# A hybrid gMLP and attention step on one core: the input projection in blocks of 512 columns, tiles at multiples of 512 bytes, and full rows for the last sample keys

## The chip, the cores and the metric

The kernel runs on one core of a Trainium2 chip. A core has a matrix engine (PE; its weight loads are shown apart as PEld), a vector engine (DVE), a scalar engine (ACT), a general engine (POOL) and a sync engine (SP) that here only starts DMAs. The metric is the device time of one execution in microseconds (us); lower is better. Several executions are timed and the median counts.

## The reference

One layer of a streaming encoder serves two groups with shared weights: a prompt of 2048 rows and 8 running streams with 16 new rows each, 128 sample rows in all. Model width is 1024, everything is fp32.

```python
h = rms_norm(x, norm_g)
z = einsum("btd,de->bte", h, w_in)                    # 1024 -> 3584 columns
u_a, v_a, g_a, q, k, v, g_b = split(z, 7 x 512)
y_a = u_a * spatial_gate(v_a) * silu(g_a)             # per 128-position chunk, lower-triangular mix, 4 heads
q, k = rms_norm(q), rms_norm(k)                       # per 64-wide half
a = softmax(Q1 K1) - lam * softmax(Q2 K2)             # 4 heads, ALiBi, block-causal in chunks of 64
y_b = rms_norm(a @ v) * silu(g_b)
y = x + concat(y_a, y_b) @ w_out
```

The prompt attends to itself. Each sample stream attends to 1024 cached keys and values and to its own 16 new ones. New keys, values and the sample's v_a rows are outputs too.

## The kernel before

**Precision.** Every fp32 operand of a product is split into a rounded high part and the rest (`split`, L136: one ACT copy, one subtraction on DVE or POOL). A product is three matmuls (`mm3`, L148): high by high, high by rest, rest by high.

**Token tiles.** Rows go in 17 tiles of 128: 0 to 15 are the prompt, 16 is the sample. `xload` and `xpose` load, normalize, transpose and split a tile into `xT`. Tiles 0 to 3 and 8 to 11 lie in the pool `p1g`, tiles 4 to 7 and 12 to 15 in the pool `p1`; the second half of the prompt takes the buffers of the first.

**Input projection.** The work is cut into 14 column blocks of 256: `v` (2), `qk` (4), `ug` and `vg` (4 each). `stream` takes all 14 blocks over tiles 0 to 7 and the sample, then all 14 over tiles 8 to 15. `load_w` (L287) brings a block's weights as 8 chunks of 128 rows by 256 columns: one DMA (two for `vg`), a scaled copy on ACT (L305), the rest on DVE (L306). Weight chunks have NW = 12 buffers, raw chunks three. `project` multiplies two token tiles by one block into one PSUM bank, 48 matmuls of 256 columns. The moving operand is the weight chunk, the stationary one is `xT`.

**Evacuation.** `qk_group`, `v_group`, `ug_group` and `vg_group` take a pair of tiles out of the bank. `vg_group` returns `finish`, the mixing product of the gMLP branch. `stream` calls the `finish` of a group of tiles right after the next group, whatever its kind. The `finish` of the sample tile appends its head to `gated_heads`.

**Order.** `weave` emits steps of two streams in a ratio of matrix-engine time that it counts in columns. The schedule is: 6 blocks of projection alone; then projection with the sample attention (ratio RS = 2.8); then, **once all four heads are in `gated_heads`**, `sample_finish` and the prompt attention of the first 8 tiles, called attention A, with projection (ratio RA = 2.0); then the output weights `wo`, in slots that attention A held; then what is left of the projection; then output projection with the attention of the other 8 tiles. A planner at compile time fixes the order of each engine's queue: it follows the order of emission, and takes a later instruction where, by its own estimate, an earlier one isn't ready.

**Attention A.** A unit is a head and a pair of query tiles, 16 units. `score_steps` cuts the keys with `chunks`: pieces of 512, except that a rest of 640 becomes 384 and 256. Exponentials of the first softmax have three buffers, of the second one. `value_steps` (L592) transposes them in PSUM (`a_tp`), splits them and multiplies (`oT`).

**Sample values.** `sample_values` multiplies 8 tiles of 128 keys and then the last 16 keys with two matmuls over 16 rows (`sO`, L830).

## Time and profile before

| | |
|---|---|
| median of 3 runs | 1416.73 us (1413.92 to 1419.37) |
| the profiled execution, from its first to its last instruction | 1410.9 us |
| what lies around it, against the median | 5.8 us |
| projection matmuls of 256 columns | 5376 on prompt tiles, 336 on the sample tile |
| output projection matmuls of 512 columns | 816 |
| mean granted clock of PE | 0.994 |

The profiled execution has no time of its own besides its span; a change of the span is carried to the median one to one. The page's slices are 35.3 us each. A matmul's shown duration includes its way through the array; the pace of a stream is found from a merged row of the timeline as (length minus one duration) over (count minus one).

### The profile page before, as it was taken

The page shows a single profiled execution, that of the slowest core. Times are in us where ns is not written, and L with a number is a line of the kernel's source. Part 1 is how long each engine was busy: PE and PEld are TensorE (multiplying, and loading weights), DVE is VectorE, ACT ScalarE, POOL GpSimd, SP SyncE. Part 2 cuts the span into 40 slices and gives each one's busy share as a digit, 9 for nine tenths or more (in the row PEclk, how much of TensorE's full clock was granted, in tenths as well). Part 3 has the DMA queues.
Part 4 walks back from the last instruction along what each step waited for, and adds up shares of the span by engine and source line. Part 5 has one row for each costly group of instructions (what it writes and reads, how often), then busy time and mean ns, then how long its engine had stood idle before and what let it go on. Part 6 is the DMA issues. An engine that isn't in the chain of part 4 may idle for free.

```text
span 1410.9 us, 27990 instructions
## 1 busy us (share of the span) xinstructions
PE 1360.5 (96%) x9892; PEld 1266.1 (90%) x9892; DVE 897.1 (64%) x2114; ACT 794.0 (56%) x1778; POOL 617.6 (44%) x796
## 2 busy tenths in 40 slices
PE   7999999999999989899999999988999999999998
PEld 6999999999999979899999999986888888888887
DVE  5442366767565764786766767444888778878632
ACT  5442356666655775565554655443777767667520
POOL 2361535555554655656232331243555545444310
PEclk9999999999999999999999999998999999999999
DMA  7533244545444476445343332166555433433223
GB/s 220 175 91 100 78 122 124 169 130 158 130 140 145 142 220 203 112 112 138 96 128 83 99 96 69 42 211 207 149 158 162 142 115 117 143 97 94 75 94 101
DMA packets 209245, 183.06 MB, mean 130 GB/s; under 512 B 21104, under 2 KB 167024, under 8 KB 209104
## 3 DMA queue, kind: packets, MB, share of 16 engines
q1 hardware_dynamic: 199280, 155.17, 36.9%
q0 software_dynamic: 9824, 26.09, 6.8%
q8 instruction: 78, 1.28, 0.4%
q14 instruction: 63, 0.52, 0.1%
HBM read 130.86 MB, written 42.47 MB: 123 GB/s over the span
## 4 chain that ended last, share of the span: by engine, by line
PE 50%; DMA 7%; DVE 5%; ACT 3%; issue 3%; POOL 3%; SPq 1%; ACTq 0%; DVEq 0%; POOLq 0%
PE acc L73 16%; PE oo L73 12%; PE S L73 8%; PE oT L73 7%; PE a_tp L77 4%; DMA wraw<-in_w_in_dram 2%; DMA svraw<-in_cache_v_dram 1%; DMA woraw<-in_w_out_dram 1%; DVE ex L584 1%; DMA x<-in_x_prompt_dram 1%; DVE ex L568 1%; PE y_tp L77 1%; DMA qraw<-q_scr 1%; POOL sv L139 1%; DVE w L306 1%
## 5 line engine op out<-in xcount | busy, mean ns | idle before, releaser
L73 PE MATMUL acc<-w,xT 128*128 128x256 f32 x5376 | 719.4, 284 | 2.5 <-DVE w L306 0.9
L73 PEld LDWEIGHTS acc<-w,xT 128*128 128x128 f32 x5376 | 676.2, 190 | 14.8 <-issue 2.7
L73 PE MATMUL oo<-wo,yT 128*128 128x512 f32 x816 | 223.6, 405 | 6.6 <-ACT yT L138 6.6
L73 PE MATMUL S<-kT,qT 128*128 128x512 f32 (+3 forms) x688 | 185.8, 367 | 6.2 <-DVE sst L568 3.9
L572 ACT ACTIVATE ex<-ex,sst 128x128 f32<-128x128 f32 (+15 forms) x128 | 153.9, 1203 | 61.0 <-DVE sst L568 59.5
L73 PEld LDWEIGHTS oo<-wo,yT 128*128 128x128 f32 x816 | 148.9, 191 | 34.7 <-ACT yT L138 7.6
L306 DVE SCALAR_TENSOR_TENSOR w<-wraw,normg,w 128x256 fp32r<-128x256 f32 x224 | 119.6, 555 | 87.1 <-ACT w L305 79.1
L305 ACT ACTIVATE w<-wraw,normg 128x256 fp32r<-128x256 f32 x220 | 105.8, 505 | 87.8 <-DMA wraw<-in_w_in_dram 75.3
L73 PE MATMUL oT<-aT,v 128*128 128x256 f32 x864 | 151.8, 290 | 2.9 <-ACT aT L138 1.9
L568 DVE CUSTOM_DVE_ANT_0 ex<-S,dist,sst 128x512 f32<-128x512 f32 (+2 forms) x192 | 123.2, 652 | 37.6 <-PE S L73 35.8
L73 PEld LDWEIGHTS oT<-aT,v 128*128 128x128 f32 x864 | 124.3, 189 | 14.5 <-DVE aT L139 3.9
L139 POOL TENSOR_TENSOR sv<-svraw,sv 128x512 fp32r<-128x512 f32 (+1 forms) x72 | 96.6, 1346 | 75.5 <-ACT sv L138 59.1
L73 PEld LDWEIGHTS S<-kT,qT 128*128 128x128 f32 x688 | 110.4, 191 | 21.3 <-DVE sst L568 8.6
L138 ACT CAST aT<-a_tp 128x512 fp32r<-128x512 f32 (+1 forms) x144 | 79.3, 559 | 70.4 <-PE a_tp L77 68.5
L139 DVE TENSOR_TENSOR aT<-a_tp,aT 128x512 fp32r<-128x512 f32 (+1 forms) x144 | 94.3, 658 | 38.2 <-ACT aT L138 37.3
L568 DVE CUSTOM_DVE_ANT_0 ex<-S,dist 128x512 f32<-128x512 f32 (+3 forms) x128 | 79.6, 629 | 29.8 <-PE S L73 16.6
L77 PE MATMUL a_tp<-ident,ex 128*128 128x128 f32 x544 | 83.1, 273 | 4.3 <-DVE ex L584 3.3
L784 POOL TENSOR_TENSOR slo<-slo,dist_s 64x256 f32<-64x256 f32 (+1 forms) x64 | 49.4, 772 | 63.3 <-ACT slo L783 60.5
L139 POOL TENSOR_TENSOR v<-vraw,v 128x512 fp32r<-128x512 f32 x36 | 48.2, 1338 | 54.5 <-ACT v L138 45.4
L77 PEld LDWEIGHTS a_tp<-ident,ex 128*128 128x128 f32 x544 | 63.3, 140 | 8.5 <-DVE gbt L641 1.9
L584 DVE SCALAR_TENSOR_TENSOR ex<-ex,sst 128x1024 f32<-128x1024 f32 (+4 forms) x64 | 65.1, 1038 | 1.1
L588 POOL TENSOR_TENSOR ex<-ex 128x1024 f32<-128x1024 f32 (+4 forms) x32 | 58.4, 1848 | 15.9 <-ACT ex L587 11.4
(144 smaller groups left out, 1925.5 us busy)
## 6 DMA issues: line engine op xcount, KB each, us to landing
wraw<-in_w_in_dram SPq DMA_DIRECT2D x160, 128.0 KB, 2.5
skraw<-in_cache_k_dram SPq DMA_DIRECT2D x64, 256.0 KB, 3.1
svraw<-in_cache_v_dram SPq DMA_DIRECT2D x64, 256.0 KB, 2.9
kT<-k_scr POOLq DMA_DIRECT2D x20, 512.0 KB, 4.6
vraw<-out_dram SPq DMA_DIRECT2D x36, 256.0 KB, 2.8
y<-y_scr SPq DMA_DIRECT2D x34, 256.0 KB, 3.0
out_dram<-xo SPq DMA_DIRECT2D x34, 256.0 KB, 2.1
wraw<-in_w_in_dram SPq DMA_DIRECT2D x128, 64.0 KB, 2.2
```

The lines of the kernel that those rows point to most:

```text
L73: pe.last = nc.tensor.matmul(*a, **k).ins
L77: pe.last = nc.tensor.transpose(*a, **k).ins
L138: act.copy(hi, src)
L139: (lo_eng or dve).tensor_tensor(out=lo, in0=src, in1=f(hi), op=ALU.subtract)
L305: act.activation(w[:, 0], r, AF.Copy, scale=normg[:, kc:kc + 1])
L306: dve.scalar_tensor_tensor(out=w[:, 1], in0=r, scalar=normg[:, kc:kc + 1], in1=f(w[:, 0]), op0=ALU.mult, op1=ALU.subtract)
L568: dve.tensor_tensor_reduce(out=ex[c][:, a:b], in0=s, in1=dist[:, off + a:off + b], scale=SLOPES[h], scalar=prev[c], op0=ALU.add, op1=ALU.m ...
L572: act.activation(ex[c][:, :w], ex[c][:, :w], AF.Exp, bias=prev[c], scale=-1.0, accum_out=st[:, c, 6:7])
L584: dve.scalar_tensor_tensor(out=p0, in0=p1, scalar=st[:, 1, 7:8], in1=p0, op0=ALU.mult, op1=ALU.add)
L588: pool.tensor_tensor(out=p0, in0=p1, in1=p0, op=ALU.add)
L784: pool.tensor_tensor(out=lo, in0=lo, in1=dist_s[rh, x:x + w_], op=ALU.add)
```

## The change

The column blocks become 512 wide: `v` for all heads (1 block), `qk` for two heads (2 blocks), `g` with u, v and both gates of one head (4 blocks). The first half runs v, qk, qk, g, g, g, g; the second v, qk, g, g, g, g, qk. One token tile by one block fills a bank: 24 matmuls of 512 columns. A weight chunk is 128 by 512, brought in two pieces, with 10 buffers instead of 12. Evacuation goes tile by tile. A `finish` is now kept in `keep["fin"]` and called by `fin()`: in `g_group` after the first tile of the next pair, and at the end of the stream. Small tiles go to a pool of their own ahead of the others, and slots are declared in an order with a filler of 480 bytes, so that the operands of most matmuls begin at multiples of 512 bytes. The 16 last sample keys are padded with zeros to 128 rows. `chunks` cuts plain pieces of 512. The last of the eight output weight chunks is loaded after the projection's pools are closed. Comment lines and docstrings are removed too.

```diff
-NW = 12             # weight chunks
+NW = 10
+    small = ctx.enter_context(tc.tile_pool(name="small", bufs=2, reuse_waits="tile"))
-    q_scr = [dtile([T + P, P], f"q_scr{h}") for h in range(H)]
+    q_scr = [dtile([T + P, 2, P], f"q_scr{hp}") for hp in range(H // 2)]
...
         def load_w(kind, h, res):
+            src = {"v": (lambda kc, i: win[kc, :, 5, 2 * i:2 * i + 2]),
+                   "qk": (lambda kc, i: win[kc, :, 3 + i, 2 * h:2 * h + 2]),
+                   "g": (lambda kc, i: win[kc, :, 0:2, h] if i == 0 else win[kc, :, 2:7:4, h])}[kind]
             for kc in range(8):
...
+                w = sb.tile([P, 2, 512], F32R, name="w", tag="w", bufs=NW)
+                for i in range(2):
+                    raw = (sb if progress[0] else at).tile([P, 2, P], F32, name="wraw", tag="wraw", bufs=3)
+                    sp.dma_start(raw, src(kc, i))
+                    r, cs = fl(raw), slice(i * 256, (i + 1) * 256)
+                    if i == 0 and not progress[0]:
+                        pool.tensor_scalar(out=w[:, 0, cs], in0=r, scalar1=normg[:, kc:kc + 1], scalar2=1.0,
+                                           op0=ALU.mult, op1=ALU.mult)
+                    else:
+                        act.activation(w[:, 0, cs], r, AF.Copy, scale=normg[:, kc:kc + 1])
+                    dve.scalar_tensor_tensor(out=w[:, 1, cs], in0=r, scalar=normg[:, kc:kc + 1],
+                                             in1=f(w[:, 0, cs]), op0=ALU.mult, op1=ALU.subtract)
...
+        def project(t, w, load):
             acc = bank("acc", "acc")
+            for kc in range(8):
+                mm3(acc, xTs[t][0][:, kc], xTs[t][1][:, kc], w[kc][:, 0], w[kc][:, 1], kc == 0, kc == 7)
+                next(load, 0)
+                sets[0] += 1
+                yield pe_time(1536) + (next(side[0], 0) if side and sets[0] % 3 == 0 else 0)
+            return acc
...
+        def g_group(h, tiles, w, loads):
+            sample = tiles[0] == NT
+            for pr in pairs(tiles):
...
+                for i, t in enumerate(pr):
+                    acc = yield from project(t, w, loads.pop(0))
...
+                    if i == 0:
+                        fin()
...
+                def finish(pr=pr, n=n, usg=usg, vhl=vhl):
...
+                    if sample:
+                        gated_heads.append(h)
+                keep["fin"] = finish
...
+            qkv = [("v", 0), ("qk", 0), ("qk", 1)]
+            gated = [("g", h) for h in range(H)]
+            kinds = qkv + gated, qkv[:2] + gated + qkv[2:]
...
-                    fin = yield from KIND[kind](h, g, w, loads)
-                    if keep.get("fin"):
-                        keep.pop("fin")()
-                    keep["fin"] = fin
+                    yield from KIND[kind](h, g, w, loads)
                 for _ in load:
                     pass
                 w = w_next
+            fin()
...
     def chunks(w, m=512):
-        res, x = [], 0
-        while w - x > m:
-            step = m - P if w - x == m + P else m
-            res.append((x, x + step))
-            x += step
-        res.append((x, w))
-        return res
+        return [(x, min(x + m, w)) for x in range(0, w, m)]
...
-            v = sa.tile([P, 2, 512], F32R, name="sv", tag="sv")[0:n]
-            split(raw, v[:, 0], v[:, 1], pool)
+            v = sa.tile([P, 2, 512], F32R, name="sv", tag="sv")
+            if n < P:
+                pool.memset(f(v), 0.0)
+            split(raw, v[0:n, 0], v[0:n, 1], pool)
...
+        pool.memset(f(aT[:, 8]), 0.0)
...
-                pe.matmul(o, lhsT=aT[0:n, kt].rearrange("p s q -> p (s q)"), rhs=vs[kt][:, i],
+                pe.matmul(o, lhsT=aT[:, kt].rearrange("p s q -> p (s q)"), rhs=vs[kt][:, i],
...
+        ctx.enter_context(tc.tile_pool(name="end", bufs=1, reuse_waits="tile", side="right")).tile(
+            [P, 120], F32, name="end", tag="end")
         bg = open_pool(right, "bg")
+        for tag, n in [(m[2], NK), (m[3], NK), (m[7], 1088), (m[11], 1088), ("dist", NK), (r[6], 544)]:
+            bg.tile([P, n], F32, name=tag, tag=tag, bufs=1)
...
-        while progress[0] < 5:
+        while progress[0] < 2:
...
-        while progress[0] < 6:
+        while progress[0] < 3:
...
-        for kc in range(8):
+        wo = [wo_tiles(wp, kc) for kc in range(7)]
+        for kc in range(7):
...
         left.close()
+        wo.append(wo_tiles(open_pool(right, "wo7", 1), 7))
+        for n in range(2):
+            raw = ypool.tile([P, 512], F32, name="woraw", tag="y", bufs=2)
+            sp.dma_start(raw, wout[7][:, n * 512:(n + 1) * 512])
+            split(raw, wo[7][n][:, 0], wo[7][n][:, 1], (pool, dve)[n])
```

231 lines of the change are left out of this document (82 added, 149 removed).

## The prediction

> **What bounds the kernel now.** I read the page first, then the busy time by stretches, then the timeline of PE, and last the timelines of ACT and SP where PE has holes. The page:
>
> ```profile
> PE 1360.5 (96%) x9892; PEld 1266.1 (90%) x9892; DVE 897.1 (64%) x2114; ACT 794.0 (56%) x1778; POOL 617.6 (44%) x796
> L73 PE MATMUL acc<-w,xT 128*128 128x256 f32 x5376 | 719.4, 284 | 2.5 <-DVE w L306 0.9
> ```
>
> PE is busy 96% of the span and no other engine over 64%. Half of that is the projection, and in all its matmuls PE stood idle for only 2.5 us. The stretches (columns: length, busy us and count of PE, PEld, DVE, ACT, POOL, granted clock, DMA share, GB/s) show the few holes:
>
> ```profile
> 498.00:545.00 47.00, 41.96 (x277) 35.66 (x276) 24.43 (x46) 31.88 (x62) 25.91 (x29) 0.96 0.79 242
> 545.00:917.00 372.00, 365.85 (x2968) 358.83 (x2968) 251.49 (x625) 201.11 (x550) 142.57 (x235) 1.00 0.36 100
> 943.00:992.00 49.00, 36.32 (x146) 27.91 (x146) 22.56 (x55) 20.08 (x36) 21.58 (x27) 0.86 0.62 193
> ```
>
> PE idles 5 us where the second half's token tiles come in, and 13 us, with the clock down to 0.86, where output projection begins. Elsewhere the end is set by how many matmuls there are, how fast they follow each other, and whether something is there to fill PE while attention waits on its own chain.
>
> **The pace of the matmuls.** Dense runs of 256 columns, then of 512 (start, length, name, count):
>
> ```profile
> 53.58 18.06 PE L73 MATMUL acc<-w,xT 128*128 128x256 f32 x153
> 122.89 3.04 PE L73 MATMUL acc<-w,xTs 128*128 128x256 f32 x24
> 125.77 22.56 PE L73 MATMUL acc<-w,xT 128*128 128x256 f32 x192
> 919.73 10.29 PE L73 MATMUL acc<-w,xT 128*128 128x256 f32 x86
> 930.54 11.67 PE L73 MATMUL acc<-w,xT 128*128 128x256 f32 x96
> ...
> 983.32 0.86 PE L73 MATMUL oo<-wo,yT 128*128 128x512 f32 x3
> ...
> 1380.51 7.94 PE L73 MATMUL oo<-wo,yT 128*128 128x512 f32 x33
> ...
> 1395.62 11.43 PE L73 MATMUL oo<-wo,yT 128*128 128x512 f32 x48
> ```
>
> With 284 ns for the last one, (18.06 - 0.284) / 152 = 117.0 ns from start to start; the others are 120, 116.6, 117.7 and 119.9. Weighted by count this is 117.9 ns, 235.8 for two. A matmul of 512 columns takes (11.43 - 0.405) / 47 = 234.6 in the longest run, 235.5 in the next, and (0.86 - 0.405) / 2 = 227.5 in the short one. So the pace is nearly proportional to columns: joining two matmuls halves the instructions but not the time. What differs is the place of the operand. The last two rows of 256 are one block's tiles 8 to 11 (117.7) and 12 to 15 (119.9, 96 = 4 x 24), the same weights with `xT` in pool `p1g` and in pool `p1`; the sample's `xTs`, a third place, runs at 120. A few per cent hang on something other than shape. New places at multiples of 512 bytes may bring the faster end, 227.5, or nothing, 235.5. I choose 229.5, three parts to one for the fast row, because the place shows in the rows and the change gives every operand the same start. 5712 matmuls become 2856: 2856 x (235.8 - 229.5) = **-18 us**, between -1 (at 235.5) and -24 (at 227.5). The same step could help the 816 output matmuls: 816 x 235 against 816 x 230 is **-4**, between 0 and -6.
>
> The Trainium skill, page "TensorE: Matmul & The Clock Gate", section "Back-to-back issue gap", gives a warm gap of N / 2.4 + 2.5 ns, thus 109.2 and 215.8; by that alone 2856 x 2.6 = 7 us would go. No row here is that fast for fp32 operands.
>
> **Padding the sample keys.** A 16-row matmul, and three full ones of the same product:
>
> ```profile
> 524.43 0.86 PE L73 MATMUL sO<-sv,saT 128*128 128x512 f32 x3
> ...
> 553.29 0.50 PE L73 MATMUL sO<-sv,saT 16*128 16x512 f32 x1
> 553.72 3.85 PE L73 MATMUL acc<-w,xT 128*128 128x256 f32 x30
> ```
>
> The next instruction starts 0.43 us after the 16-row one, and 0.23 after a full one. There are 16: -0.2 x 16 = **-3**. The added memsets (two in each of 8 batches; the trace's largest POOL memset, 1040 elements, takes 0.96 us) lie on POOL, busy under 60% of any stretch, hidden by projection. Without that cover they would cost 8 x 1.1 = 9; I keep -5 to +2.
>
> **Key pieces.** Only a rest of 640 was cut otherwise: 3 query tiles x 4 heads x 2 softmaxes = 24 times. A third of these has one small matmul pair less. I take **-1**, between -3 and 0, as the columns are the same.
>
> **Token tiles of the second half.** They are transposed beside the last block of the first half, now twice as long per group. Of the 5 us idle in 498 to 545, with its clock of 0.96, I take **-4** (-7 to 0). At the very start the first block needs 2 MB of weights, not 1, but also gives twice the matmuls per token tile: **+2** (-3 to +7).
>
> **Weights with fewer buffers.** The rows around a change of block, ACT and SP:
>
> ```profile
> 915.53 1.31 ACT L305 ACTIVATE w<-wraw,normg 128x256 fp32r<-128x256 f32 x3 [1.04 <-PE acc L73]
> 918.72 0.51 ACT L305 ACTIVATE w<-wraw,normg 128x256 fp32r<-128x256 f32 x1
> ...
> 916.59 0.33 SPq L291 DMA_DIRECT2D wraw<-in_w_in_dram  x1
> ```
>
> Three raw pieces lie ready when buffers come free; the fourth comes 3.2 us after the first, as its DMA waits for a raw buffer. Before, 4 of 8 pieces came this late way, that is two rounds. Now 12 of 16 do, four rounds, the last one 3 x 3.2 = 9.6 us after the first, while the last token tile gives 24 x 0.23 = 5.5 us. The next block's last chunks come 2 to 5 us late. The planner has covered that so far by taking the next tile's first chunks (2.5 us of idle in all), and two banks allow it again. I take **+2** for 13 changes of block, and keep 0 to +25 (13 x 2). ACT and DVE do the same number of columns; their few more small instructions have DVE's 36% of idle time as cover. Stores of q, k and v stay about as many on SP.
>
> **Attention A starts later.** This is the step that speaks against the change. The counts of projection matmuls, in the same columns as above, for these instructions alone:
>
> ```profile
> 0.00:553.70 553.70, 442.22 (x3312) 416.04 (x3312) 23.34 (x60) 38.93 (x96) 1.00 0.49 148
> 553.70:913.90 360.20, 293.14 (x2175) 275.53 (x2176) 19.59 (x47) 24.42 (x61) 1.00 0.36 99
> 913.90:943.00 29.10, 27.25 (x227) 27.00 (x225) 0.41 (x1) 2.40 (x5) 1.00 0.64 192
> ```
>
> Sample attention ends at 553.7 with 3312 - 3024 = 288 of the second half's 2688 matmuls done. All gates are then complete and attention A follows at once. After the change the last sample head's `finish` hangs on the next `g` block, and that comes after v and qk of the second half: 2 x 8 + 1 tiles, 816 matmuls of the old size. The loop that waits for `gated_heads` emits 816 - 288 = 528 of them alone, 62 us, ahead of attention A. What is left for it as filler is 1872. Attention A took 360 us with 2175, 6.04 per us; 1872 last 310 us. So some 50 us of it run with nothing beside, and the output weights, which wait for its slots, lose the 227 matmuls that covered them. How slow is it alone?
>
> ```profile
> 897.14 0.60 PE L77 MATMUL a_tp<-ident,ex 128*128 128x128 f32 x4
> ...
> 901.60 0.60 PE L77 MATMUL a_tp<-ident,ex 128*128 128x128 f32 x4
> 901.96 0.85 PE L73 MATMUL oT<-aT,v 128*128 128x256 f32 x5
> 902.65 2.64 PE L73 MATMUL acc<-w,xT 128*128 128x256 f32 x21
> 905.12 0.28 PE L73 MATMUL oT<-aT,v 128*128 128x256 f32 x1
> 905.24 0.87 PE L73 MATMUL acc<-w,xT 128*128 128x256 f32 x6
> 905.95 0.49 PE L77 MATMUL a_tp<-ident,ex 128*128 128x128 f32 x3
> ```
>
> A step of values takes 4.4 us, of which the 27 projection matmuls are 3.2; without them it is bound by transposes, split and product, some 2.3 us. So the bare 50 us shrink to about 26. Their own PE work is (360 - 2175 x 0.118) / 360 x 50 = 14. That leaves 12 us of idle PE: **+12**, between 0 (if attention A gets ahead in the gaps of those 62 us) and +36 (if its chain keeps its pace). The loads of the output weights:
>
> ```profile
> 941.67 1.14 ACT L138 CAST wo<-woraw 128x512 fp32r<-128x512 f32 x2 [2.90 <-DMA woraw<-in_w_out_dram]
> 945.79 1.14 ACT L138 CAST wo<-woraw 128x512 fp32r<-128x512 f32 x2 [2.98 <-DMA woraw<-in_w_out_dram]
> 947.32 0.59 ACT L138 CAST yT<-y_tp 128x512 fp32r<-128x512 f32 x1
> 947.95 2.07 PE L73 MATMUL oo<-wo,yT 128*128 128x512 f32 x4 [5.31 <-ACT yT L138]
> ```
>
> They come 4 us apart. Seven after attention A would be 28 us bare, but the second attention's first loads need only the projection's pools, now free earlier, and can fill the 13 us that are idle there today. I take these as even, **0**, between -8 and +15.
>
> **The sum.** -18 - 4 - 3 - 1 - 4 + 2 + 2 + 12 = -14 on a span of 1410.9, thus 1397; with the 5.8 us around it, 1403 against the median of 1416.7, -1.0%.
>
> **The rivals.**
> 1. Attention A pays in full: its tail at +36, the output weights at +15. Against the sum that is 24 + 15 = 39: **1442**. From 14 of these 39 on the kernel is no faster than before; that is where attention A outlasts its filler by some 40 us. For it speaks the 62 us; against it that a planner's order without filler runs as fast as its data allow.
> 2. The pace doesn't move: 235.5 for 512 columns, output matmuls unchanged. 17 + 4 us are lost again: **1424**. The two longest runs of 512 speak for it; the short one against. The Trainium skill, page "SBUF — State Buffer", section "Operand start alignment", asks of an fp32 operand only that it starts at a multiple of its element size, and says of this that it is about legality, not speed; it names no larger step at which an operand gets faster, and by it alone this rival would be the likeliest.
> 3. The fast pace everywhere, 227.5 or below, and attention A hidden: -6 - 2 - 12, **1383**.
>
> **How the numbers follow.** Forecast 0.44 (its own range 1390 to 1413), rival 1 0.2, rival 2 0.16, rival 3 0.2. About 0.5%, 7 us, is what a measurement of this kernel can tell from no change. Below 1409.6 fall rival 3 and some three quarters of the forecast: 0.53. Above 1423.8 most of rival 1 and half of rival 2: 0.25. Range 1380 to 1432: it holds the forecast and rival 3 nearly whole, rival 2, and the cheaper third of rival 1.
>
> **What would show it.** The pace of 512-column projection matmuls in dense runs (229 right; 235 is rival 2). A stretch of some 60 us of projection alone after the last sample product, and whether the last projection matmul stands before or after the last `o_tp` of attention A. Idle PE before `oo`, and whom it waits for. Idle PE before `acc` with DVE `w` as the releaser, over 10 us, would prove the weights late. The 16-row gaps gone. The forecast is wrong if sample or attention stages change their length for a cause not listed here.

## The result and the profile after

| | before | after |
|---|---|---|
| median | 1415.39 us (4 runs) | 1503.22 us (4 runs, 1498.78 to 1504.47) |
| ratio | | **1.0615**, 95% interval 1.0587 to 1.0643 |
| span of the profiled execution | 1410.9 us | 1500.5 us |
| mean granted clock | 0.994 | 0.962 |
| projection matmuls | 5712 of 256 columns | 2856 of 512 columns |

The kernel became 6% slower, where 1% faster was forecast; the time lies far above the range's end of 1432. From the page after:

```profile
PE 1381.5 (92%) x7036; PEld 1137.7 (76%) x7036; DVE 907.6 (60%) x2170; ACT 792.8 (53%) x1805; POOL 637.6 (42%) x850
...
PEclk9999999999999899999998888988999999999999
...
L73 PE MATMUL acc<-w,xT 128*128 128x512 f32 x2688 | 679.1, 400 | 14.0 <-DVE usg L369 5.6
```

PE was busy 96% of the span and is now busy 92%; the clock falls below nine tenths in the 14th, the 22nd to the 25th and the 27th and 28th of the slices of 37.5 us. The idle time ahead of the projection's matmuls went from 2.5 to 14.0 us. The largest named part, 5.6 us, is put down to `usg`, the last step that reads a gated bank; 3.5 us are put down to the weights `w`.

The same stages in both kernels, cut at the first sample score, the last sample product and the last projection matmul (columns as in the prediction). Before:

```profile
0.00:195.00 195.00, 184.69 (x1533) 183.02 (x1534) 84.79 (x186) 82.23 (x170) 76.63 (x95) 1.00 0.44 131
195.00:553.00 358.00, 348.30 (x2707) 329.42 (x2706) 234.16 (x523) 232.00 (x559) 189.35 (x217) 1.00 0.52 157
553.00:942.00 389.00, 382.85 (x3106) 375.58 (x3105) 260.94 (x632) 207.07 (x564) 151.04 (x242) 1.00 0.38 105
942.00:1410.90 468.90, 444.66 (x2554) 378.07 (x2553) 317.20 (x773) 272.66 (x486) 200.56 (x242) 0.99 0.43 129
```

After:

```profile
0.00:203.00 203.00, 185.84 (x832) 149.14 (x833) 93.95 (x194) 78.37 (x168) 84.41 (x103) 0.99 0.43 133
203.00:572.00 369.00, 348.54 (x1828) 288.77 (x1827) 233.17 (x538) 233.77 (x568) 198.11 (x244) 0.99 0.49 146
572.00:643.00 71.00, 62.28 (x273) 49.97 (x272) 41.42 (x86) 33.34 (x85) 35.65 (x41) 0.94 0.46 135
643.00:1024.00 381.00, 338.84 (x1586) 276.48 (x1585) 220.50 (x579) 174.41 (x500) 117.67 (x218) 0.90 0.29 81
1024.00:1500.50 476.50, 446.06 (x2525) 373.33 (x2523) 318.60 (x775) 272.93 (x485) 201.73 (x245) 0.98 0.43 128
```

Of the 89.6 us, 8 came in the stage of lone projection, 11 beside the sample attention, **63 in the stage of attention A** (71 + 381 against 389) and 7.6 in output projection. In the worst stretch, 643 to 1024, PE is idle for 42 us and its clock is 0.90. No engine but PE is busy for more than 58% of it. The matmuls themselves got faster. Dense runs after, one on `xT`, one on `xTs`, and the longest of output projection:

```profile
76.78 39.60 PE L73 MATMUL acc<-w,xT 128*128 128x512 f32 x174
116.22 5.60 PE L73 MATMUL acc<-w,xTs 128*128 128x512 f32 x24
...
1485.60 11.18 PE L73 MATMUL oo<-wo,yT 128*128 128x512 f32 x48
```

With 400, 392 and 404 ns for the last one: 39.20 / 173 = 226.6 ns, 5.21 / 23 = 226.5 and 10.78 / 47 = 229.3. Two of 256 had taken 235.8, and `oo` 234.6. So some 2856 x 9.2 = 26 us of matmul time went, and about 115 us came from elsewhere.

**Where PE stands still.** PE in attention A, after (start, length, name, count):

```profile
810.73 1.77 PE L73 MATMUL acc<-w,xT 128*128 128x512 f32 x7
...
826.58 1.12 PE L77 MATMUL a_tp<-ident,ex 128*128 128x128 f32 x4 [1.11 <-DVE gbt L606]
...
832.35 4.28 PE L73 MATMUL acc<-w,xT 128*128 128x512 f32 x17
```

For 20 us no projection matmul is issued. What attention issues there has small waits between, and an `a_tp` of four takes 1.12 us, where the prediction's rows had 0.60: from 824 to 830 us the granted clock is 0.50. Why is there no projection? ACT in the same stretch:

```profile
806.05 0.39 ACT L366 ACTIVATE sg<-acc 128x256 f32<-128x256 f32 x1 [0.54 <-PE acc L73]
...
824.61 0.20 ACT L600 ACTIVATION_READ_ACCUMULATOR os<-o_tp 128x1 f32 x1
824.71 0.30 ACT L377 ACTIVATE junk<-vn 128x128 f32<-128x128 f32 x1
...
828.21 0.41 ACT L136 CAST vhl<-vn 128x256 fp32r<-128x256 f32 x1
829.40 0.43 ACT L367 COPY vn<-acc 128x128 f32<-128x128 f32 x2 [0.78 <-DVE vhl L137]
```

and DVE:

```profile
826.98 0.61 DVE L382 SCALAR_TENSOR_TENSOR vn<-vn,vst,sgug 128x128 f32<-128x128 f32 x2
...
828.96 0.41 DVE L137 TENSOR_TENSOR vhl<-vn,vhl 128x256 fp32r<-128x256 f32 x1
...
831.17 0.28 DVE L369 SCALAR_TENSOR_TENSOR usg<-sg,acc 128x128 f32<-128x128 f32 x1
```

The tile whose gate starts at 806.05 has its `vn` copied out of the bank at 829.40, 23 us later; where nothing holds it, the copy follows the gate by 0.3 us. It waits because there is one `vn` buffer and the pair before still holds it: its squares (824.71), its normalization (826.98) and its split (828.21, 828.96) come late. The squares stand on ACT right behind the statistics of attention's output (824.61). Until `usg` at 831.17 the bank is full, the second tile's bank as well, and there are only two.

**The weights.** ACT and SP at a change of block in attention A, after:

```profile
858.14 1.31 ACT L298 ACTIVATE w<-wraw,misc 128x256 fp32r<-128x256 f32 x3 [1.36 <-PE acc L73]
861.39 1.54 ACT L298 ACTIVATE w<-wraw,misc 128x256 fp32r<-128x256 f32 x3 [1.95 <-DMA wraw<-in_w_in_dram]
864.70 0.51 ACT L298 ACTIVATE w<-wraw,misc 128x256 fp32r<-128x256 f32 x1 [1.40 <-DMA wraw<-in_w_in_dram]
...
865.56 0.51 ACT L298 ACTIVATE w<-wraw,misc 128x256 fp32r<-128x256 f32 x1
...
866.71 0.51 ACT L298 ACTIVATE w<-wraw,misc 128x256 fp32r<-128x256 f32 x1
...
869.95 0.51 ACT L298 ACTIVATE w<-wraw,misc 128x256 fp32r<-128x256 f32 x1
...
870.75 0.89 ACT L298 ACTIVATE w<-wraw,misc 128x256 fp32r<-128x256 f32 x2
```

SP there:

```profile
859.19 9.44 SPq L292 DMA_DIRECT2D wraw<-in_w_in_dram  x9
```

These are the twelve late pieces of one block: three lie ready at 858.14, and nine more DMAs follow. The first three rounds start as forecast, 3.25 us apart. The last piece starts 13 us after the first (871.15), not 9.6. Its round was slowed by ACT, which had attention's work to do up to 869.95, while the first piece of that round had landed at 867.86. Over the twelve blocks of this run whose pieces all go through ACT, the late ones take 11 to 21 us from the first start to the last.

### The profile page after: what moved, and what is told of

It reads as the page before. It is cut to its first block, busy times and chain, and to the rows that moved or that the text cites. A ratio compares the mean times of both kernels' runs of the same rounds, so it can differ in the third digit from the quotient of the medians.

```text
span 1500.5 us, 22434 instructions
## 1 busy us (share of the span) xinstructions
PE 1381.5 (92%) x7036; PEld 1137.7 (76%) x7036; DVE 907.6 (60%) x2170; ACT 792.8 (53%) x1805; POOL 637.6 (42%) x850
## 4 chain that ended last, share of the span: by engine, by line
PE 54%; DMA 14%; DVE 11%; ACT 8%; issue 7%; POOL 5%; SPq 1%; DVEq 0%; ACTq 0%; POOLq 0%
PE acc L73 23%; PE oo L73 10%; DMA wraw<-in_w_in_dram 7%; PE S L73 6%; PE oT L73 5%; PE a_tp L77 3%; DVE w L299 2%; POOL qst L144 2%; ACT w L298 2%; ACT ex L537 2%; DVE ex L533 1%; DMA vraw<-out_dram 1%; DVE ex L549 1%; PE sO L73 1%; PE sS L73 1%
## 5 line engine op out<-in xcount | busy, mean ns | idle before, releaser
L73 PE MATMUL acc<-w,xT 128*128 128x512 f32 x2688 | 679.1, 400 | 14.0 <-DVE usg L369 5.6
L73 PEld LDWEIGHTS acc<-w,xT 128*128 128x128 f32 x2688 | 502.5, 192 | 123.2 <-ACT w L298 4.7
L73 PE MATMUL oT<-aT,v 128*128 128x256 f32 x864 | 160.2, 301 | 7.8 <-ACT aT L136 7.0
L299 DVE SCALAR_TENSOR_TENSOR w<-wraw,misc,w 128x256 fp32r<-128x256 f32 x224 | 115.6, 536 | 83.4 <-ACT w L298 68.2
L298 ACT ACTIVATE w<-wraw,misc 128x256 fp32r<-128x256 f32 x208 | 100.9, 505 | 100.6 <-DMA wraw<-in_w_in_dram 85.8
L73 PEld LDWEIGHTS oT<-aT,v 128*128 128x128 f32 x864 | 130.6, 198 | 25.3 <-ACT aT L136 11.4
L137 POOL TENSOR_TENSOR sv<-svraw,sv 128x512 fp32r<-128x512 f32 (+1 forms) x72 | 93.0, 1300 | 49.5 <-ACT sv L136 41.4
L77 PE MATMUL a_tp<-ident,ex 128*128 128x128 f32 x544 | 88.3, 283 | 13.3 <-DVE gbt L606 9.4
L544 POOL TENSOR_SCALAR sst<-sst 128x1 f32<-128x1 f32 x64 | 17.6, 275 | 137.6 <-ACT ex L537 131.7
L372 POOL TENSOR_TENSOR gb<-sg,subg 128x128 f32<-128x128 f32 x68 | 32.8, 487 | 87.5 <-DVE sg L368 79.1
```

Of the source, the lines that this page charges most:

```text
L73: pe.last = nc.tensor.matmul(*a, **k).ins
L77: pe.last = nc.tensor.transpose(*a, **k).ins
L137: (lo_eng or dve).tensor_tensor(out=lo, in0=src, in1=f(hi), op=ALU.subtract)
L298: act.activation(w[:, 0, cs], r, AF.Copy, scale=normg[:, kc:kc + 1])
L299: dve.scalar_tensor_tensor(out=w[:, 1, cs], in0=r, scalar=normg[:, kc:kc + 1], in1=f(w[:, 0, cs]), op0=ALU.mult, op1=ALU.subtract)
L372: pool.tensor_tensor(out=gb, in0=sg[:, 1], in1=subg, op=ALU.mult)
```

## Experiments

Three theories at the start. **W**: the weights come late. **F**: attention A starts too late, as the prediction feared. **G**: 512 columns a step and the longer evacuation leave attention A no filler. Two more came on the way: **S** (a shared ring of slots) and **A** (the projection runs too far ahead). Ratios are to the kernel before, run on the same chips, with the 95% interval. Beside these runs the kernel before stood at 1410.9 to 1412.7 us, beside the change at 1415.4. Where the change is compared with a run below, it is therefore taken as 1.0615 x 1412 = 1499 us.

### One load of weights, after and before

```diff
-                load = load_w(*blocks[n + 1][2:], w_next) if n + 1 < len(blocks) else iter(())
+                load = iter(())
...
-                w = w_next
+                w = w_next or w
```

> The changed kernel with the weights of the first block kept for all 14 blocks: 13 of 14 loads are left out, with their 208 DMAs and 416 instructions on ACT and DVE, so that most columns of the projection are those of other weights. Theory W (the 86 us lost after the last sample product are weights that come late, through two spare chunks and three raw buffers): all of it comes back, 1395 to 1415 us. Theory F (attention A begins too late because the last sample head is finished one block later): its start stays behind the second half's first gated tile, so 1460 to 1500. Theory G (512 columns a step and a longer evacuation leave attention A without filler between its steps): 1460 to 1500 as well, since steps and evacuation stay.

> The same leaving out in the kernel before, as the control of the run above: one load of weights, kept for all 28 blocks, the rest of the loads left out. There PE waited 2.5 us ahead of projection matmuls, so every theory expects 1400 to 1417 us, within 1% of the kernel before. If it falls by far more than that, loading costs time in the kernel before too and the run above can't be read as what the change added.

After: **1447.54 us**, 1.0258 (1.0233 to 1.0283). Before: **1404.18**, 0.9945 (0.9926 to 0.9964). The time after lies between what W and what F and G gave. In the kernel before, loading costs 7 us. In the changed one it costs some 51 (1499 - 1448), but 43 us against the control remain, so W alone falls, and so do F and G as sole causes. A run with one load leaves out the work of loading too, on ACT, DVE and the DMA queues, and not only the lateness. All that remains lies in one stage. After with one load, from the last sample product to the last projection matmul:

```profile
545.40:973.30 427.90, 388.76 (x1832) 316.48 (x1831) 219.72 (x577) 172.35 (x499) 149.66 (x258) 0.93 0.23 67
```

Before with one load:

```profile
548.60:933.80 385.20, 384.38 (x3133) 378.84 (x3133) 222.94 (x544) 169.28 (x474) 152.88 (x246) 1.00 0.27 76
```

39 us of idle PE instead of 1, at a clock of 0.93, without any weight to wait for. In this run, too, gated tiles stay in their banks for up to 24 us.

### The shared ring

The diff has one more line that the long form above leaves out:

```diff
-        st = sb.tile([P, 2, 2], F32, name="ost", tag="ost", bufs=2)
+        st = small.tile([P, 2, 2], F32, name="ost", tag="vst", bufs=3)
```

`ost` holds the statistics of an attention unit's output, `vst` those of a gated pair. In the changed kernel both take three slots of one tag in turn, so that a pair's squares can have to wait until an attention unit has given its slot back. Theory S: this ring ties the projection's banks to attention's pace, through `vst`, the squares and the one `vn` buffer. Undone at the same number of bytes:

```diff
-                st = small.tile([P, 2, 2], F32, name="vst", tag="vst", bufs=3)
+                st = small.tile([P, 2, 2], F32, name="vst", tag="vst", bufs=2)
...
-        st = small.tile([P, 2, 2], F32, name="ost", tag="vst", bufs=3)
+        st = small.tile([P, 2, 2], F32, name="ost", tag="ost", bufs=1)
```

> The changed kernel with the statistics of attention's output (ost) on a tag of their own again: one slot for ost and two for vst, in place of three that both take in turn; the bytes stay the same. Theory S, new after the run that keeps one load of weights: in attention A the squares of a gated pair run only behind the statistics of an attention unit, because both take slots of one ring; until then the one vn buffer isn't free, so the next pair's bank isn't read (15 to 25 us after its tanh in place of 0.3), and with two banks the projection stands. With a ring of its own that wait goes and some 40 us come back, 1455 to 1475; what is left over the kernel before are the weights. Theory V (the one vn buffer alone is too few, whatever the ring): the banks are still held, 1490 to 1505. Theory W alone: 1490 to 1505.

> The changed kernel with the weights of the first block kept for all blocks (13 of 14 loads left out, most columns of the projection are those of other weights), and ost on a tag of its own. Theories S and W together: nothing is left of the loss, 1390 to 1410, that is at or below the 1404 of the kernel before with one load. Theory V, or a third cause such as 512 columns a step: 1430 to 1450, as with one load and the shared ring.

And the ring alone put into the kernel before:

```diff
+    small = ctx.enter_context(tc.tile_pool(name="small", bufs=2, reuse_waits="tile"))
...
-                st = sb.tile([P, 2, 2], F32, name="vst", tag="vst")
+                st = small.tile([P, 2, 2], F32, name="vst", tag="vst", bufs=3)
...
-        st = sb.tile([P, 2, 2], F32, name="ost", tag="ost", bufs=2)
+        st = small.tile([P, 2, 2], F32, name="ost", tag="vst", bufs=3)
```

> The kernel before with nothing changed but the ring: vst and ost take three slots of one tag in turn, as in the changed kernel. There the bank is read into va, of which there are two, and not into vn, so a bank is held only from the third pair on. Theory S: the squares stand behind attention's statistics here too and some of the loss appears, 1425 to 1450. If the ring costs only together with the single vn buffer that the bank is read into: 1408 to 1418.

Own ring: **1480.74**, 1.0487 (1.0460 to 1.0513). Own ring and one load: **1430.16**, 1.0121 (1.0092 to 1.0149). The ring in the kernel before: **1461.92**, 1.0345 (1.0315 to 1.0376), which is **+49 us** from the ring alone, 12 above the range expected (two slots for each of the two tiles became three for both in turn; that three kept apart are enough, the run with its own ring shows). In its attention A, 550 to 1000 us, the banks hold up the projection as they do after:

```profile
L73 PE MATMUL acc<-w,xT 128*128 128x256 f32 x2424 | 318.8, 285 | 10.9 <-DVE sg L370 5.1 <-DVE usg L379 4.9 <-DVE w L307 0.9
```

In the changed kernel with its own ring, ACT copies and squares at once:

```profile
722.36 0.38 ACT L366 ACTIVATE sg<-acc 128x256 f32<-128x256 f32 x1 [1.05 <-PE acc L73]
722.64 0.26 ACT L367 COPY vn<-acc 128x128 f32<-128x128 f32 x1
722.93 0.31 ACT L377 ACTIVATE junk<-vn 128x128 f32<-128x128 f32 x1
```

Every copy in attention A follows its gate by 0.3 to 0.6 us. The number of `vn` buffers is still one, so theory V falls. But only 18 us came back where some 40 were expected, and the run with one load missed what S and W together forecast. The stage shows why. Own ring, all loads, to the last projection matmul and then to the output projection:

```profile
570.60:921.70 351.10, 336.92 (x1652) 280.20 (x1651) 216.58 (x548) 170.82 (x483) 127.36 (x211) 0.98 0.34 99
921.70:1010.00 88.30, 53.86 (x226) 40.83 (x226) 51.62 (x119) 39.88 (x103) 30.76 (x51) 0.69 0.27 81
```

Now the projection is done at 922 and attention A runs alone until 992. PE is idle for 34 of the 88 us, at a clock of 0.69: 22 us while attention A runs bare, and 12 in one wait for `y_scr` behind it. The loss has moved from "projection can't run" to "no projection is left".

### The finish of the sample heads

```diff
                     yield from KIND[kind](h, g, w, loads)
+                    if last and not half:
+                        fin()
```

> The changed kernel with the pending finish of a sample head called right behind the sample rows' group, so that the last sample head no longer waits for the second half's first gated tile. Theory F: attention A's first scores start at about 545 instead of 588 us, and some 40 of the 88 us come back, 1455 to 1470. Theory W: the first scores start earlier, but 1141 matmuls of projection still stand beside attention A or behind it and stall on weights as before; the 45 us of projection that runs alone at its end only grows: 1485 to 1510.

> The changed kernel with ost on a tag of its own and the sample heads' finish called right behind the sample rows' group. Theory F, in a new form: with the ring undone the projection no longer stalls in attention A, ends at 922 us and leaves attention A alone to 1005, where PE idles and its clock falls, since attention A began at 585 to 640 with 62 us of projection spent alone ahead of it. An earlier finish gives that projection back to attention A as filler: 1481 - 40 = 1440, between 1425 and 1455. Theory W alone (only late weights are left): the finish changes nothing, 1470 to 1490.

Alone: **1512.09**, 1.0712 (1.0693 to 1.0731), some 13 us slower than without the edit. With the own ring: **1476.47**, 1.0456 (1.0430 to 1.0482), 4 us better than without; the intervals overlap. F's forecasts (1455 to 1470, and 1425 to 1455) fail in both forms. The first score came at 576 and 582 us instead of 588 and 585, so little was gained at the start. The rest shows when the projection matmuls still to come (in 512 columns) are counted at the end of attention A's units:

| kernel | at the first score | unit 4 | unit 8 | unit 12 | unit 16 |
|---|---|---|---|---|---|
| before | 1238 | 872 | 619 | 367 | 114 |
| before, shared ring | 1238 | 872 | 672 | 606 | 480 |
| after | 1104 | 672 | 480 | 336 | 192 |
| after, early finish | 1122 | 864 | 768 | 576 | 480 |
| after, own ring | 1104 | 598 | 235 | 0 | 0 |
| own ring, early finish | 1122 | 706 | 390 | 5 | 0 |

In the kernel before the filler lasts. With the ring, put into it or after, the filler is held back, at the price of idle PE; with the early finish alone it is held back more than after, and one copy of `vn` came 54 us behind its gate. With a ring of its own it is gone by unit 12.

With one load of weights the same edit does more. Own ring and one load took 1430.16 us, and with the early finish 1412.32 (next section): **18 us**, with intervals that don't touch. There the step is seen as the prediction described it. Without the edit, 55 us of projection and almost nothing else on PE stand between the last sample product and the first score:

```profile
546.10:601.00 54.90, 54.90 (x249) 45.53 (x248) 18.19 (x35) 16.50 (x42) 29.32 (x33) 1.00 0.23 74
```

With it, the first score comes 3 us behind the last sample product:

```profile
547.68 0.22 PE L73 MATMUL S<-kT,qT 128*128 128x128 f32 x1
```

The filler left at the first score grows from 877 to 1115. So F is a cause, but with all loads most of it doesn't show: there the first score stands only 16 us behind the last sample product (587.6 and 571.8 after), with 1104 matmuls left.

### How far the projection may run ahead

`weave` lets the projection's PE instructions run at most AA steps of attention ahead of their place, AA = 100 in both kernels. The planner puts a ready projection ahead of an attention step that it takes to be not ready, so theory A is that with the ring undone this limit is too wide.

```diff
-RA, AA = 2.0, 100
+RA, AA = 2.0, 38
```

With own ring, early finish and one load, without and with the limit:

> The changed kernel with the weights of the first block kept for all blocks (13 of 14 loads left out, most columns of the projection are those of other weights), ost on its own tag, and the early finish. Theories S, F and W together: nothing is left of the loss, and the gain of pace shows: 1385 to 1402, below the 1404 of the kernel before with one load. A fourth cause: 1415 to 1430.

> The changed kernel with one load of weights (13 of 14 left out, most columns of the projection are those of other weights), ost on its own tag, the early finish, and the projection held to at most 38 attention steps ahead instead of 100. In the order of PE's instructions 82 projection matmuls are then left when attention A's last unit ends, where with 100 none are left from the 12th of 16 units on (before: 114 of that size). Theory A (the projection runs ahead and leaves attention A bare): the 8 us to the kernel before with one load and the gain of pace come back, 1385 to 1400. If something else of the change makes attention A slow: 1405 to 1420.

And with all loads:

> The changed kernel with ost on its own tag, the early finish and the limit of 38, and all loads of weights. Theory A: 1476 less the 15 to 25 us that the run with one load gains by the limit, 1450 to 1462; what is left over that run is then the price of the late weights, 55 to 65 us. If late weights need the projection to run ahead: no gain, 1470 to 1490.

At 100: **1412.32**, 0.9995 (0.9980 to 1.0009), between the two ranges expected. At 38: **1388.57**, 0.9842 (0.9813 to 0.9871), which is 16 us below the kernel before with one load. With all loads: **1439.88**, 1.0212 (1.0185 to 1.0238), 37 us better than at 100 and 10 better than the best expected. With one load, at 100, until the last projection matmul and until output projection:

```profile
545.00:881.40 336.40, 334.37 (x1700) 281.59 (x1699) 188.21 (x498) 147.53 (x432) 133.81 (x228) 1.00 0.24 69
881.40:937.60 56.20, 30.16 (x143) 21.82 (x141) 34.16 (x75) 25.27 (x61) 19.84 (x30) 0.79 0.29 89
```

At 38, the whole stage:

```profile
542.10:908.00 365.90, 358.87 (x1835) 299.74 (x1834) 216.93 (x565) 167.28 (x488) 142.73 (x251) 1.00 0.25 72
```

At 38 the counts of the table are 1115, 879, 720, 495 and 82, and the stretch of 56 us with a clock of 0.79 is gone. Theory A holds. The limit was not tried without the early finish and all else equal, nor in the kernel before. With one load, the projection's part ends 26 us earlier than in the control (908.0 against 933.8), which is what the pace should give; the output stage behind it then takes 9 us longer (478.4 against 469.1).

### What the late weights cost, and where

The run with the limit and all loads is 1439.88 - 1388.57 = **51 us** above the one with one load. This is the price of loading, work and lateness together, once the ring, the finish and the limit are out of the way. The limit with all loads, in the same stages as above:

```profile
0.00:202.90 202.90, 185.51 (x833) 149.43 (x834) 93.34 (x194) 78.23 (x168) 85.27 (x103) 0.99 0.43 133
202.90:568.00 365.10, 347.08 (x1829) 288.38 (x1827) 235.25 (x537) 233.28 (x565) 198.58 (x245) 0.99 0.49 149
568.00:958.90 390.90, 372.48 (x1857) 305.58 (x1856) 263.97 (x662) 209.25 (x587) 148.86 (x254) 0.99 0.36 104
```

With one load the three took 194.5, 347.6 and 365.9 us: the weights cost 8.4 us ahead of the first sample score, 17.5 beside the sample attention and 25 in attention A's stage.

The first tries were made on the changed kernel with its ring (7 raw buffers for 3) and with the own ring. The 4 KB for them came from the token tiles of the second half:

```diff
-            x = (at if t < 8 or t == NT else sb).tile([P, D], F32, name="x", tag="x", bufs=2)
+            x = (at if t < 8 or t == NT else sb).tile([P, D], F32, name="x", tag="x", bufs=1)
...
-                    raw = (sb if progress[0] else at).tile([P, 2, P], F32, name="wraw", tag="wraw", bufs=3)
+                    raw = (sb if progress[0] else at).tile([P, 2, P], F32, name="wraw", tag="wraw", bufs=7)
...
-            raw = p1.tile([P, D], F32, name="woraw", tag="x", bufs=2)
+            raw = p1.tile([P, D], F32, name="woraw", tag="x", bufs=1)
```

> The changed kernel with 7 instead of 3 raw buffers for the weights, paid for with one instead of two buffers for a token tile of the second half (and for the output weights on the way in), which by itself can cost 5 to 10 us where the second half's tiles come in. Theory W with the raw buffers as the narrow place (the rounds of three DMAs, each 3.2 to 3.3 us, and the stores of attention A between them on SP's queue): 1420 to 1460. Theory W with the two spare chunk buffers as the narrow place: 1480 to 1510, no better than before the edit. Theories F and G: 1495 to 1515.

> The changed kernel with ost on a tag of its own and 7 raw buffers in place of 3, paid for with one buffer for a token tile of the second half instead of two. If the ring and the late weights are two causes that add up: 1503 - 40 - 32 = 1431, between 1420 and 1445. If both only hold the same projection in the same stretches: no better than the better of the two alone, 1455 to 1470.

**1471.41**, 1.0435 (1.0412 to 1.0457), some 28 us better than the change; and **1464.56**, 1.0372 (1.0342 to 1.0403), 16 better than own ring alone. The first lies between what the theories gave, the second in the range for two causes that hold the same projection (1455 to 1470); they don't add up (1431 was wanted). In the first the ring still holds the filler back: 192 matmuls are left after the last unit. In the second none is left at unit 12, and what the projection gains is lost again when attention A runs bare. What the one `x` buffer costs by itself was not tried. The same holds, with none left at unit 12, for own ring, early finish, 6 raw buffers, one `x` buffer, and a tag of its own for `junk`:

```diff
-                    junk = sb.tile([P, P], F32, name="junk", tag="z")
+                    junk = sb.tile([P, P], F32, name="junk", tag="junk", bufs=1)
```

> The changed kernel with ost on its own tag, the early finish, 6 raw buffers in place of 3, and the output of the gated squares on a tag of its own (it shared the slots of z with the token tiles' squares, and in the stretch where the second half's tiles come in a bank was held for 24 us, 42 with seven raw buffers), paid for with one buffer for a token tile of the second half. Theories S, F and W add up: 1395 to 1420, about the kernel before. If the one token-tile buffer costs more than the raw buffers bring: above 1430.

**1469.09**, 1.0412 (1.0384 to 1.0441): 50 us above the range of the sum, and above 1430 as if the one token-tile buffer cost more than the raw buffers bring; which of the two it is, the run can't tell. Where the second half's tiles come in, a bank was still held for 31 us (24 in the change, 42 with 7 raw buffers), so the slots of `z` are at most a part of that hold; its cause stays open.

With the limit at 38 but without the early finish, chunks that come free more slowly: the last two tiles of a block share each chunk, and the sample rows go ahead of tiles 4 to 7. (The loading and the second half's token tiles move along with them, in lines that the form below leaves out.)

```diff
+            ts = [t, t + 1] if t in (6, 14) else [t]
+            accs = [bank("acc", "acc") for _ in ts]
             for kc in range(8):
+                for u, a in zip(ts, accs):
+                    mm3(a, xTs[u][0][:, kc], xTs[u][1][:, kc], w[kc][:, 0], w[kc][:, 1], kc == 0, kc == 7)
                 next(load, 0)
...
-            halves = [[[0, 1, 2, 3], [4, 5, 6, 7], [NT]], [[8, 9, 10, 11], [12, 13, 14, 15]]]
+            halves = [[[0, 1, 2, 3], [NT], [4, 5, 6, 7]], [[8, 9, 10, 11], [12, 13, 14, 15]]]
```

> The changed kernel with ost on its own tag, the limit of 38, the sample rows' group ahead of tiles 4 to 7 in the first half (which finishes the sample heads one tile later), and the last two token tiles of every block taken chunk by chunk into the two banks, so that the chunks come free over 11 us instead of 5.5. Theory W: the 12 late pieces need some 13 us at 3 pieces in 3.25 us; instead of 7.5 us about 2 us a change of block are missing, plus up to 1.5 us in which both banks are read: 13 x 4 = 52 us of the run before fall to 25 to 45, 1415 to 1440. If it isn't the time in which chunks come free: 1450 to 1465.

**1441.79**, 1.0218 (1.0194 to 1.0241): no gain over 1439.88, and between the two ranges. The edit takes both banks at once, and what it may gain seems to be paid there; as three things were changed together, this is argued and not shown. Projection from 30 to 1000 us in this run, where the run with the limit alone has 10.1 us of idle time and `usg` is not among its first three reasons:

```profile
L73 PE MATMUL acc<-w,xT 128*128 128x512 f32 x2630 | 662.0, 399 | 13.2 <-DVE usg L375 9.0 <-ACT w L298 2.3 <-ACT z L331 1.6
```

The kernel before with two spare chunks instead of four:

```diff
-NW = 12             # weight chunks
+NW = 10
```

> The kernel before with 10 instead of 12 weight chunks, all else as it was: 2 instead of 4 of a block's 8 chunks can be loaded ahead, as in the changed kernel, but a chunk is half as large, so 6 pieces come late in a change of block, not 12. Theory W: 6 pieces through 3 raw buffers are two rounds, the last some 4 us behind its place at most; 26 changes x 0.5 to 2 us, 1425 to 1465. If the kernel's order covers late weights as long as the ring isn't shared: 1408 to 1420.

**1435.27**, 1.0175 (1.0154 to 1.0196): +24 us for two buffers of 2 KB of each partition, in a kernel where loading had cost 7. Last, chunk buffers traded for raw buffers, four raw for each:

```diff
-NW = 10
+NW = 8
...
-                    raw = (sb if progress[0] else at).tile([P, 2, P], F32, name="wraw", tag="wraw", bufs=3)
+                    raw = (sb if progress[0] else at).tile([P, 2, P], F32, name="wraw", tag="wraw", bufs=11)
```

> The changed kernel with ost on its own tag, the early finish, the limit of 38, and one chunk buffer (4 KB of each partition) traded for four raw buffers: 9 chunks, 7 raw. If the raw buffers are the narrow place: 7 pieces lie ready when chunks come free and the rounds of 3.25 us shrink from four to two, 1405 to 1430 against 1440. If the spare chunks are: 14 instead of 12 of 16 pieces come late and it costs 5 to 20, 1445 to 1460.

> The same with a second chunk buffer traded: 8 chunks, none of them spare, and 11 raw. If the raw buffers are the narrow place: 11 of 16 pieces lie ready and only ACT's and DVE's work is late, 1400 to 1430. If the spare chunks are: all 16 pieces come late, 1460 to 1490.

9 and 7: **1417.71**, 1.0033 (1.0007 to 1.0060). 8 and 11: **1414.64**, 1.0014 (0.9995 to 1.0033). So, with the limit and the own ring, the raw buffers were the narrow place, not the chunks: with fewer chunks and more raw buffers, 25 of the 51 us go. ACT's weight pieces over the whole run, with the limit and 3 raw buffers:

```profile
L298 ACT ACTIVATE w<-wraw,misc 128x256 fp32r<-128x256 f32 x208 | 100.9, 506 | 88.4 <-DMA wraw<-in_w_in_dram 83.2 <-PE acc L73 4.2
```

with 8 chunks and 11 raw buffers:

```profile
L298 ACT ACTIVATE w<-wraw,misc 128x256 fp32r<-128x256 f32 x208 | 89.9, 499 | 14.7 <-DMA wraw<-in_w_in_dram 13.1 <-PE acc L73 1.2
```

ACT's wait for raw pieces falls from 83 to 13 us. This version equals the kernel before; none that computes everything beats it. The 26 us left above the run with one load were not split further.

### Where operands begin

With own ring and early finish (1476.47 us), a filler of 64 bytes ahead of the pool `p1`. It moves `w` and `xT` 64 bytes off their multiples of 512; `xTs` stays.

```diff
+        sb.tile([P, 16], F32, name="pad", tag="pad", bufs=1)
```

> The changed kernel with ost on its own tag and the early finish, and the weights' chunks and the prompt's transposed token tiles moved by 64 bytes, so that both begin 64 bytes behind a multiple of 512; the sample rows' xTs stay at a multiple. If the pace hangs on where operands begin, projection matmuls of 512 columns on xT go from 227 ns back to 234 to 240 start to start, while those on xTs keep xT's offset of the other operand alone and lie between; 2688 x 0.007 to 0.013 = 19 to 35 us of work come back. If the pace hangs on 512 columns a matmul alone, it stays at 227.

**1478.95** in one run. The dense runs:

```profile
75.86 39.60 PE L73 MATMUL acc<-w,xT 128*128 128x512 f32 x174
115.30 5.66 PE L73 MATMUL acc<-w,xTs 128*128 128x512 f32 x24
```

39.20 / 173 = 226.6 ns on `xT`, the same as without the shift; 5.27 / 23 = 229 on `xTs` (in three runs of 24), 2.5 ns slower, where one operand is moved and the other isn't. So this shift doesn't bring the old pace back. Other offsets were not tried.

The run with the ring in the kernel before says more than it was made for. Its pool of small tiles lies ahead of all others and moves what comes behind it; the shapes stay:

```profile
124.45 2.97 PE L73 MATMUL acc<-w,xTs 128*128 128x256 f32 x24
...
1433.23 7.76 PE L73 MATMUL oo<-wo,yT 128*128 128x512 f32 x33
```

The same rows of the kernel before, in the prediction, took 3.04 and 7.94 us. So 256 columns on `xTs` went from 120 to 116.8 ns, and 512 columns of `oo` from 235.5 to 229.9, by place as far as the run can tell; `xT` became slower, 119.3 in the run of 192 that had 116.6. By how many bytes the tiles moved was not worked out, so which places are fast stays open.

## Why the prediction was wrong, point by point

**What was forecast and came.** The pace: 229.5 ns chosen, 226.6 measured, 26 us instead of 18. The five rows of 256 columns weigh to 117.6 ns by count, not 117.9, so the pace term should have read -16; the measured gain is then 25. The output matmuls: 229.3 where 230 was taken, in the longest run, 816 x 5.3 = 4 us, as forecast if all gained as much. The gap behind 16-row matmuls is gone: after, the instruction behind a last sample product starts 0.23 us later, as behind any other.

```profile
571.82 0.40 PE L73 MATMUL sO<-sv,saT 128*128 128x512 f32 x1
572.05 1.30 PE L73 MATMUL acc<-w,xT 128*128 128x512 f32 x5
```

All 24 key pieces that were cut otherwise lost a pair of matmuls (`S` has 640 instead of 688), not a third of them. What these two and the second half's token tiles brought in time was not measured on their own. Together with the pace they are the 26 us by which the projection ends earlier with one load and the limit.

**The reason given for the pace was right in part.** The prediction held that joining two matmuls doesn't shorten the time and that the place of the operands does. Place counts: in the kernel before with the ring, `xTs` and `oo` became 2 to 3% faster and `xT` 2% slower, with their shapes unchanged. But multiples of 512 bytes are not what does it, as 64 bytes of shift of both operands left `xT` at 226.6. That both operands have the same start, which the prediction also named, is not refuted: where the shift broke it, on `xTs`, the pace fell to 229. And joining saves something: the fastest rows of 256 columns, 116.6 ns, give 233.2 for two, 6.6 more than one of 512. How the 9 ns between 235.8 and 226.6 divide was not settled, and that the pace came out even better than chosen is in part luck. The rule of the Trainium skill that was weighed there (page "TensorE: Matmul & The Clock Gate", section "Back-to-back issue gap": N / 2.4 + 2.5 ns) gives 2.5 ns a pair, 2.6 with the prediction's rounding, and 215.8 ns; neither number shows here. The Trainium skill's other rule (page "SBUF — State Buffer", section "Operand start alignment") is, in its own words, about legality and not speed, and nothing was timed for it; so rival 2 gains nothing from it.

**The weights: +2 taken, some 44 measured**, beyond the bound of +25. Loading costs 51 us in the changed kernel and 7 in the kernel before. The count of late pieces (12 of 16 in rounds of three) was right. Two steps failed. "[T]he last one 3 x 3.2 = 9.6 us after the first" supposed that the rounds follow each other undisturbed; it was 11 to 21 us, as a raw buffer comes free only when ACT and DVE have done the piece, and they have other work between. And "the planner has covered that so far" was carried over to three times as many late pieces for each change of block; even in the kernel before two spare chunks fewer cost 24. The sign that was named for it, idle PE ahead of `acc` with `w` as the releaser for over 10 us, never appeared: it was 3.5 us in the change and 6.0 in the run with the limit. The order on PE is fixed, so we read it that the wait falls on whoever stands next in it; what showed the price were the runs without loads.

**Attention A starts late: +12 taken, 18 measured with one load, little with all.** With one load and the own ring, 55 us of projection alone (62 forecast) stand ahead of attention A, and the early finish brings 18 us. With all loads the prediction's other case came: attention A got ahead while the projection was held up, and its filler at the first score was 1104 matmuls, 2208 of the old size, where 1872 were forecast. The step's consequence, a filler that runs out, did not happen in the changed kernel: 192 matmuls were left after the last unit. The shared ring kept it back. With the ring undone the filler does run out, by unit 12, and there finishing the heads early brings 4 us and limiting the projection 37. So how the planner spends the filler counts for more than the start. The prediction took the filler's rate from the kernel before (6.04 matmuls per us) as if the planner had to keep it.

**The missing term.** The ring of `vst` and `ost` is in the diff and in no step of the prediction. Alone it costs the kernel before 49 us. The step that failed first is the sum's claim to be complete: every edit was costed by its instructions, and this one has none. Its wait was put at nothing; undone, it gives back 18 us in the changed kernel, and the limit's 37 us were measured only with the ring undone. "Evacuation goes tile by tile" was taken as free, although the bank is now read straight into `vn`, of which there is one buffer (before, into `va`, of which there were two), so that a late chain behind `vn` holds the bank itself.

**Output weights and the last stage: 0 taken, +7.6 in the change**, inside the bounds of -8 to +15. Of these, 5.6 us lie between the last projection matmul and the first `oo` (1023.9 to 1035.6 after, 941.9 to 948.0 before). There PE waits for the transposed rows' load:

```profile
1033.82 1.09 PE L77 MATMUL y_tp<-ident,y 128*128 128x128 f32 x4 [9.21 <-DMA y<-y_scr]
```

What makes the stage longer in the other runs was not tried.

In sum: 1499 with the change, beside a kernel before of 1412; 1481 with a ring of its own; 1476 with the early finish; 1440 with the limit; 1415 with raw for chunk buffers. With one load the same edits go from 1448 to 1430, 1412 and 1389. The rival "attention A pays in full" (1442) had the stage right and the mechanism wrong.

## What to carry to other kernels

A tag shared by two streams is a wait between them: list every tile whose tag or pool changes, with who gives its slot back, even when it has 16 bytes. Where two streams are woven, undoing one stall can move the loss to the end of the filler, so look after each edit at how much filler is left at every unit, and set again the limit that says how far it may run ahead. When the blocks of a loaded operand double, count the late pieces for each change of block and follow them through the buffers and engines that they pass; raw buffers can be worth more than buffers of the finished operand (25 us here, at equal bytes).

## What the runs showed of the hardware

fp32 matmuls of 512 columns follow each other every 226.6 ns, where two of 256 took 235.8. Moving weights and token tiles by 64 bytes left that at 226.6; with only one of the two operands moved it was 229. With shapes unchanged and tiles moved by a pool ahead of them, 256 columns went from 120 to 116.8 ns and 512 from 235.5 to 229.9. Matmul streams with waits between them lost clock: while attention A ran bare, in 70 us with 48 us of PE work and no wait over 3.9 us, the granted clock was 0.73 (own ring, 922 to 992 us). In the change, four transposes at a granted clock of 0.50 took 1.12 us, where 0.60 was the time before.
